# Part of a decoder block's input projection as a Strassen stage of its own, ahead of attention

## The chip, the cores and the metric

The kernel runs on one core of a Trainium2 chip. The metric is the time of one execution in microseconds on the device, as the median of several runs. The core has TensorE (PE: matmuls, with weight loads as PEld), VectorE (DVE), ScalarE (ACT), GpSimd (POOL) and queues that issue DMAs (SP's most of all). Each engine takes its instructions in the order in which they were put into its queue.

## The reference

One layer on 1024 tokens and 16 meta tokens of width 1024, in float32. Only the first part of it is changed, the mixer's input projection and what uses it:

```python
def hybrid_mixer(xn, w_in, conv_w_mix, w_proj_conv, w_proj_attn, b_gate, w_out):
    h = xn @ w_in                      # 1024 x 8192
    b_c, c_c, h_c, q, k, v, g_conv, g_attn = jnp.split(h, list(splits), axis=-1)
    y_conv = b_c * causal_dwconv(c_c * h_c, conv_w_mix)
    branch_conv = y_conv @ w_proj_conv
    o = stick_breaking_attention(q.reshape(hd), k.reshape(hd), v.reshape(hd))
    branch_attn = o.reshape(bsz, seq_len, D_ATTN) @ w_proj_attn
    gate_conv = jax.nn.sigmoid(g_conv + b_gate[0])
    gate_attn = jax.nn.sigmoid(g_attn + b_gate[1])
    merged = gate_conv * branch_conv + gate_attn * branch_attn
    return merged @ w_out
```

Attention has 16 heads of 64 and queries in blocks. For a query, the weight of an earlier key is the sigmoid of its score times the product of one minus sigmoid over all keys between them. Behind the mixer come a norm, a gated MLP (up and gate projections with 2816 channels each, a convolution over 3 tokens, a down projection), and a norm.

## The kernel before

Weights are laid out in blocks of 128 output channels; `w_in` has 64 such blocks: 8 each of b, c and h of the convolution, of q, k, v, and of two gates. Each fp32 value is split into a rounded part `hi` and a rest `lo` (`split`: ACT copies, DVE or POOL subtracts), and a product is three matmuls, hi x hi, hi x lo and lo x hi.

Start: nine `x_block` calls normalise 128 tokens each, transpose them on PE and split them into `xnT` (hi and lo, 8 channel blocks, 1040 tokens). Between them begin the first two blocks of the projection.

The class `Dense` works through a list of items, one item a block of weights. For each it loads `raw` (SP), makes `whi` (ACT) and `wlo` (POOL, four pieces), and goes in three chunks of some 342 tokens through 8 channel blocks, three matmuls each: 72 matmuls a block (lines 129 to 131). One step is three matmuls. A chunk's PSUM result goes to the item's `evac`. For q that is a copy on ACT and a cast and a subtraction on DVE for each of two heads (`qh`, `ql`), for k a copy and a subtraction (`kk`), for v a copy `vt`, later transposed to tokens (`vv`). Convolution items give `cc` and `yy`, gates `gt`; results that are used later are written to DRAM (`y_d`, `gc_d`, `ga_d`).

Attention runs over 8 pairs of heads, 2 heads, 3 groups `g` of three query blocks of 114. `stage1` makes scores `z` in PSUM (two buffers) for 114 queries and 128 to 1040 keys; ACT makes two sigmoids, `fl` and `be`; DVE scans `fl` along the keys (line 340); POOL multiplies it into `be` (line 346) and masks it (`affine_select`, line 348). `stage2` goes through the key blocks of a group: transposes of `be` on PE into `tp` (line 377, two buffers), ACT's copy `ah`, DVE's rest `al`, and two products `av` (lines 367, 368). A loop alternates the two stages by a table of costs, with `stage1` some 2500 units ahead, and spreads the projection's steps over them: `marks[p]` says how many items must be done when pair p is. Before, the list was v, q, k of pair 0, and then for each pair its three convolution items, one gate (four for the last) and v, q, k of the next pair. Five gates were left for after the loop.

The code is written in this order, but a scheduler moves instructions within each engine's queue at compile time; so what stands in a queue is shown below as it was compiled.

Then follow the products with `yT` and `oT` (the two branches), the output projection, the up and gate projections, and the down projection. The up and gate projections are already done in Strassen's scheme (in Winograd's form with 7 products), in pairs of weight blocks (lines 863 to 867), for tokens in even and odd columns.

Of the kernel before, what the change touches and what calls it, by code (L numbers as in the profile page):

```python
# [33 lines left out]
def block_kernel(ctx, tc, x, meta_tokens, g_pre_mix, w_in, channels, w_proj_conv,  # L34
# [32 lines left out]

    def rstd_of(small, ssq, n):
# [12 lines left out]
    class Dense:  # L81


        def __init__(self, pspool, items):
            self.ps = pspool
            self.items = items
            self.raw, self.hl = {}, {}
            self.i, self.gen, self.total, self.later = 0, None, 0, []

# [6 lines left out]

        def load(self, i):
            if i < len(self.items) and i not in self.raw and i not in self.hl:
# [5 lines left out]
        def prep(self, i):  # L104
            if i < len(self.items) and i not in self.hl:
# [35 lines left out]
        def step(self):  # L141
            while self.i < len(self.items):
# [17 lines left out]
    def col_block(w, c):  # L160
# [110 lines left out]

    def items_conv(cb):
        st = {}

        def evac_c(ci, a, n, ps):
            if ci == 0:
                st["c"] = work.tile([P, NT], F32, name="cc", tag="wk", bufs=4)
            nc.scalar.copy(st["c"][:, a - 12:a - 12 + n], ps)

        def evac_h(ci, a, n, ps):  # L280
            c = st["c"][:, a - 12:a - 12 + n]
            nc.vector.tensor_tensor(c, c, ps, op=ALU.mult)
            if ci == 2:
                st["y"] = work.tile([P, NT], F32, name="yy", tag="wk", bufs=4)
# [24 lines left out]
    gp = {"p": work, "n": 4}  # L309
# [91 lines left out]
    gate_items = [item_gate(1, ob) for ob in range(8)] + [item_gate(0, ob) for ob in range(8)]  # L401
    n_gate = [1, 1, 1, 1, 1, 1, 1, 4]
    items, marks = [], []
    items += [item_v(0), item_q(0), item_k(0)]
    gi = 0
    for p in range(NPAIR):
        items += items_conv(p)
        for _ in range(n_gate[p]):
            items.append(gate_items[gi])
            gi += 1  # L410
# [3 lines left out]
    items += gate_items[gi:]  # L414
    n_gates = len(items)
    dense = Dense(ps_mm, items)

    def start_items(x_block):
# [11 lines left out]
        chunk(0, 9)  # L430
        chunk(1, 9)
# [803 lines left out]
```

## Time and profile before

| | us |
|---|---|
| runs: median of 3 (lowest, highest) | 2024.38 (2021.74, 2027.97) |
| profiled execution, its own time | 2019.99 |
| its span in the profile | 2018.2 |
| PE busy in the span | 1968.4 |
| attention: first z to last av | 66.0 to 967 |

The profiled execution ran at a mean granted TensorE clock of 0.993. A row of groups shows line, engine, operation, out<-in, shape, count, then busy us and mean ns of one, then the engine's idle time before and what released it. A row of windows shows for each engine the busy us and, in brackets, the number of instructions. Rows of one tile give ns as least/median/greatest and the first and last start.

### The profile page before, as it was taken

How to read it: one execution, taken by the hardware profiler on the slowest of the kernel's cores; microseconds unless marked ns; L12 is line 12 of the kernel's file. 1: busy time of each engine (PE TensorE's matmuls, PEld its weight loads, DVE VectorE, ACT ScalarE, POOL GpSimd, SP SyncE). 2: the span in 40 equal slices, each digit the busy share in tenths (PEclk: the TensorE clock that was granted, in tenths of full speed). 3: DMA queues.
4: the chain of work that ended last, by engine and by line, in shares of the span. 5: the costliest groups of instructions: out<-in, count | busy, mean ns of one | idle time of the engine just before them, and what ended most of it. 6: DMA issues, size and time to landing. Idle time of an engine off the chain costs nothing.

```text
span 2018.2 us, 30990 instructions
## 1 busy us (share of the span) xinstructions
PE 1968.4 (98%) x12228; PEld 1857.0 (92%) x12228; DVE 1006.3 (50%) x1545; ACT 853.3 (42%) x1771; POOL 1022.7 (51%) x1062
## 2 busy tenths in 40 slices
PE   6999999999999999999999999979999999999997
PEld 6999999999999999999999999969988998888886
DVE  6445555555555555553341126874354445345546
ACT  5544555555454545555421123453443344321122
POOL 2643666565555646565223550345556565654353
PEclk9999999999999999999999999989999999999998
DMA  3111101111111111012664673303121212253223
GB/s 137 43 63 43 53 32 64 43 53 43 42 53 43 58 39 62 32 64 73 189 221 156 188 214 114 97 31 126 63 84 67 102 66 82 92 174 111 84 84 136
DMA packets 56174, 177.58 MB, mean 88 GB/s; under 512 B 12872, under 2 KB 12872, under 8 KB 56028
## 3 DMA queue, kind: packets, MB, share of 16 engines
q1 hardware_dynamic: 52704, 165.09, 24.5%
q10 hardware_dynamic: 3324, 10.50, 1.7%
q8 instruction: 96, 1.57, 0.3%
q14 instruction: 50, 0.41, 0.1%
HBM read 131.36 MB, written 44.21 MB: 87 GB/s over the span
## 4 chain that ended last, share of the span: by engine, by line
PE 87%; DVE 7%; ACT 2%; DMA 2%; POOL 1%; issue 1%; ACTq 0%; DVEq 0%; SPq 0%; POOLq 0%
PE mm L129 14%; PE mm L130 14%; PE mm L131 14%; PE st L863 7%; PE st L867 7%; PE st L865 7%; PE tp L377 3%; PE st L1157 3%; PE st L1155 3%; PE st L1156 3%; PE av L368 2%; PE av L367 2%; PE z L331 2%; PE z L330 2%; PE po L706 1%; PE po L708 1%
## 5 line engine op out<-in xcount | busy, mean ns | idle before, releaser
L129 PE MATMUL mm<-xnT,whi 128*128 128x342 f32 (+2 forms) x1536 | 505.5, 329 | 0.3 <-ACT xnT L65 0.2
L130 PE MATMUL mm<-xnT,whi 128*128 128x342 f32 (+2 forms) x1536 | 494.0, 322 | 0.5 <-DVE xnT L66 0.5
L131 PE MATMUL mm<-xnT,wlo 128*128 128x342 f32 (+2 forms) x1536 | 492.3, 320 | 0.0
L346 POOL TENSOR_TENSOR be<-be,fl 114x271 f32<-114x271 f32 (+14 forms) x288 | 206.0, 736 | 310.3 <-DVE fl L340 301.6
L113 POOL TENSOR_TENSOR wlo<-raw,whi 128x256 fp32r<-128x256 f32 x320 | 254.8, 828 | 208.2 <-ACT whi L110 207.3
L130 PEld LDWEIGHTS mm<-xnT,whi 128*128 128x128 f32 x1536 | 291.0, 189 | 2.1 <-DVE xnT L66 1.0
L129 PEld LDWEIGHTS mm<-xnT,whi 128*128 128x128 f32 x1536 | 290.2, 189 | 2.9 <-ACT xnT L65 0.8
L131 PEld LDWEIGHTS mm<-xnT,wlo 128*128 128x128 f32 x1536 | 290.0, 189 | 0.0
L340 DVE TENSOR_TENSOR_SCAN fl<-fl,upper 114x128 f32<-114x128 f32 (+2 forms) x144 | 214.4, 1490 | 112.2 <-ACT fl L332 64.0
L66 POOL TENSOR_TENSOR a_op<-raw,a_op 128x512 fp32r<-128x512 f32 (+1 forms) x136 | 193.7, 1437 | 87.9 <-ACT a_op L65 85.6
L66 DVE TENSOR_TENSOR al<-tp,ah 114x342 fp32r<-114x342 f32 (+3 forms) x288 | 128.3, 452 | 148.8 <-ACT ah L65 147.5
L65 ACT CAST ah<-tp 114x342 fp32r<-114x342 f32 (+3 forms) x288 | 113.0, 398 | 165.3 <-PE tp L377 157.0
L863 PE MATMUL st<-opT,a_op 128*128 128x258 f32 (+2 forms) x528 | 172.3, 326 | 3.2 <-ACT snap L878 1.8
L865 PE MATMUL st<-opT,a_op 128*128 128x258 f32 (+2 forms) x528 | 170.1, 322 | 2.6 <-DVE opT L66 1.7
L867 PE MATMUL st<-opT,a_op 128*128 128x258 f32 (+2 forms) x528 | 170.0, 322 | 0.0
L332 ACT ACTIVATE fl<-z 114x348 f32<-114x348 f32 (+10 forms) x240 | 111.4, 464 | 123.6 <-PE z L331 93.5
L65 ACT CAST a_op<-raw 128x512 fp32r<-128x512 f32 (+1 forms) x136 | 85.1, 634 | 156.0 <-DMA raw<-in_w_up_gate_dram 51.8
L1162 DVE TENSOR_TENSOR acc<-acc,st 128x512 f32<-128x512 f32 x144 | 98.5, 687 | 91.1 <-PE st L1157 91.1
L865 PE MATMUL st<-opB,a_op 128*128 128x512 f32 (+2 forms) x396 | 127.6, 322 | 0.0
L863 PE MATMUL st<-opB,a_op 128*128 128x512 f32 (+2 forms) x396 | 127.6, 322 | 0.0
L867 PE MATMUL st<-opB,a_op 128*128 128x512 f32 (+2 forms) x396 | 127.2, 321 | 0.0
L377 PE MATMUL tp<-ident,be 114*114 114x114 f32 (+1 forms) x720 | 118.5, 262 | 4.1 <-DVE al L66 3.4
(168 smaller groups left out, 4320.5 us busy)
## 6 DMA issues: line engine op xcount, KB each, us to landing
raw<-in_w_in_dram SPq DMA_DIRECT2D x64, 512.0 KB, 3.3
raw<-in_w_up_gate_dram SPq DMA_DIRECT2D x44, 512.0 KB, 3.3
act_d<-owork SPq DMA_DIRECT2D x22, 512.0 KB, 4.3
araw<-act_d SPq DMA_DIRECT2D x22, 512.0 KB
raw<-in_w_down_dram SPq DMA_DIRECT2D x22, 512.0 KB, 3.3
y_d<-yy SPq DMA_DIRECT2D x8, 513.0 KB
ga_d<-gt SPq DMA_DIRECT2D x8, 513.0 KB
o_d<-ot SPq DMA_DIRECT2D x8, 513.0 KB
```

Of the source, the lines that this page charges most:

```text
L65: nc.scalar.copy(hi, src)
L66: (lo_engine or nc.vector).tensor_tensor(lo, src, hi.bitcast(F32), op=ALU.subtract)
L113: nc.gpsimd.tensor_tensor(lo[:, c], raw[:, c], hi[:, c].bitcast(F32), op=ALU.subtract)
L129: nc.tensor.matmul(ps, wh, xh, start=(kb == 0), stop=False)
L130: nc.tensor.matmul(ps, wh, xl, start=False, stop=False)
L131: nc.tensor.matmul(ps, wl, xh, start=False, stop=(kb == KB - 1))
L340: nc.vector.tensor_tensor_scan(fl[:, :nk][:, ::-1], fl[:, :nk][:, ::-1], upper[:, NT - nk:][:, ::-1], 1.0, op0=ALU.mult, op1=ALU.max)
L346: nc.gpsimd.tensor_tensor(be[:, a:e], be[:, a:e], fl[:, a + 1:e + 1], op=ALU.mult)
L377: nc.tensor.transpose(tp[:n, QB * j:QB * (j + 1)], blocks[j][0][:, k0:k0 + n], ident[:QB, :QB])
L863: nc.tensor.matmul(ps, wt[:, 0, k], xh, start=start and kb == 0, stop=False, skip_group_check=True)
L865: nc.tensor.matmul(ps, wt[:, 0, k], xl, start=False, stop=False, skip_group_check=True)
L867: nc.tensor.matmul(ps, wt[:, 1, k], xh, start=False, stop=stop and kb == 3, skip_group_check=True)
```

## The change

30 of the 64 blocks leave the list: the convolution's blocks 1 to 7 (21), all 8 of the second gate and one of the first. They are computed in 15 pairs of blocks in the same scheme of 7 products, as a stage between the start and attention. The scheme halves channels (two halves of 512) and tokens (two halves of 520, `HT`): B11, B21, B22 are quarters of `xnT` itself, T1 to T4 are differences of quarters, made once by `token_ops`; A11, A12, A22 and S1 to S4 are made for each pair from two blocks of weights by `weight_ops`. `strassen` runs the 7 products for 260 tokens at a time, 12 matmuls each, with ACT copying three of the partial sums (`snap`) and DVE adding them. A pair is computed for all 1040 tokens. The convolution's first block (c, h, b) is done the old way at the start, in place of v, q, k of pair 0, which now follow the stage. Beside attention stand the other v, q, k and three gates; four gates are left for after the loop. Pools of SBUF and PSUM are opened and closed for the stage.

The diff, cut to its core:

```diff
+ps0 = ctx.enter_context(ExitStack())
+ps_mm0 = ps0.enter_context(pool("ps_mm0", 4, space=PSUM))
+ps_tp0 = ps0.enter_context(pool("ps_tp0", 4, space=PSUM))
...
-    n_gate = [1, 1, 1, 1, 1, 1, 1, 4]
-    items, marks = [], []
+    n_gate = [0] * 7 + [3]
+    std_gates = [item_gate(0, ob) for ob in range(1, 8)]
+    items, marks = items_conv(0), []
+    n_early = len(items)
     items += [item_v(0), item_q(0), item_k(0)]
     for p in range(NPAIR):
-        items += items_conv(p)
         for _ in range(n_gate[p]):
...
+    def token_ops():
+        for kb in range(4):
+            a, b = wk_tile("xa"), wk_tile("xb")
+            nc.vector.tensor_tensor(a, xnT[:, 0, kb].bitcast(F32), xnT[:, 1, kb].bitcast(F32), op=ALU.add)
+            nc.gpsimd.tensor_tensor(b, xnT[:, 0, kb + 4].bitcast(F32), xnT[:, 1, kb + 4].bitcast(F32),
+                                    op=ALU.add)
+            e1, o1, e2, o2 = a[:, :HT], a[:, HT:], b[:, :HT], b[:, HT:]
+            sub(nc.vector, o1, o1, e1)
+            split_top("T1", kb, o1)
+            sub(nc.vector, o1, o2, o1)
+            split_top("T2", kb, o1)
+            sub(nc.vector, e1, o1, e1)
+            split_top("T3", kb, e1)
+            sub(nc.vector, e2, e2, o1)
+            split_top("T4", kb, e2)
+            yield
...
+    for i in range(2):
+        next(tops_gen)
+        start_chunk(i, 9)
     dense.i, dense.total = 2, 48
-    dense.until(3)
...
+    load_early(0)
+    prep = prep_early(0)
+    for k in range(3):
+        dense.chunk()
+        next(tops_gen, None)
+        next(prep)
+    dense.until(n_early)
...
+    for i in range(len(early_pairs)):
+        prep = iter(()) if last else prep_early(i + 1)
+        tiles = [wk_tile("su") for _ in range(2)]
+        for si in range(2):
+            n = HT // 2
+            j0 = si * n
...
+            for k, _ in enumerate(strassen(early_ops[i], moving, n, bank_s, snaps_e,
+                                           early_evac(i, tiles, j0, n))):
+                if (7 * si + k) % 2:
+                    next(prep, None)
...
+    psS.close()
+    t_ctx.close()
+    early_ctx.close()
+    psA = ctx.enter_context(ExitStack())
...
+    dense.until(n_early + 3)
```

`weight_ops` and the order of the 7 products are those of the up projection (`prep_pair`, `products`); `early_evac` adds a result into one of two tiles `su` of 1040 tokens, and `done_c`, `done_h`, `done_b` and `done_gate` finish a block: c x h on POOL and the three convolution taps, the product with b on DVE, the sigmoid on ACT, and the DMA.

The queues at three places. First DVE just behind the last split of `xnT` at the start. Before:

```order
L230 CAST qh_348<-mm_468 64x342
L231 TENSOR_TENSOR ql_350<-mm_468,qh_348 64x342
L230 CAST qh_347<-mm_553 64x342
L231 TENSOR_TENSOR ql_349<-mm_553,qh_347 64x342
L66 TENSOR_TENSOR vv_552<-tp_598,vv_552 128x8x64
```

Now (xa and xb are the sums hi + lo of a slice of xnT, tT1 to tT4 the token operands):

```order
L433 TENSOR_TENSOR xa_502<-xnT_86 128x1040
L433 TENSOR_TENSOR xa_544<-xnT_86 128x1040
L69 TENSOR_TENSOR xa_502<-xa_502 128x520
L69 TENSOR_TENSOR xa_544<-xa_544 128x520
L66 TENSOR_TENSOR tT1_498<-xa_502,tT1_498 128x520
L69 TENSOR_TENSOR xa_502<-xb_503,xa_502 128x520
L69 TENSOR_TENSOR xa_502<-xa_502 128x520
L69 TENSOR_TENSOR xb_503<-xb_503,xa_502 128x520
L66 TENSOR_TENSOR tT2_499<-xa_502,tT2_499 128x520
L66 TENSOR_TENSOR tT3_500<-xa_502,tT3_500 128x520
L66 TENSOR_TENSOR tT4_501<-xb_503,tT4_501 128x520
L66 TENSOR_TENSOR tT1_498<-xa_544,tT1_498 128x520
```

The evacuations of q, and v's split, have given way to the token operands; 45 rows pass from the first of these to the last split of T4, with the convolution of block 0 and the first weight sums among them.

Second, DVE at the three longest scans of a head in the middle of attention. Before:

```order
L395 TENSOR_TENSOR ot_4879<-av_5438,ot_4879 64x342
L340 SCALAR_TENSOR_TENSOR fl_5502<-fl_5502,upper_93 114x812
L230 CAST qh_5460<-mm_5472 64x342
L231 TENSOR_TENSOR ql_5462<-mm_5472,qh_5460 64x342
L230 CAST qh_5461<-mm_5472 64x342
L231 TENSOR_TENSOR ql_5463<-mm_5472,qh_5461 64x342
L340 SCALAR_TENSOR_TENSOR fl_5540<-fl_5540,upper_93 114x926
L230 CAST qh_5460<-mm_5533 64x342
```

Now:

```order
L66 TENSOR_TENSOR vv_8321<-tp_8322,vv_8321 128x8x64
L399 TENSOR_TENSOR ot_8331<-av_8288,ot_8331 64x342
L66 TENSOR_TENSOR vv_8321<-tp_8347,vv_8321 128x8x64
L66 TENSOR_TENSOR vv_8321<-tp_8368,vv_8321 114x2x64
L344 SCALAR_TENSOR_TENSOR fl_8354<-fl_8354,upper_4080 114x812
L344 SCALAR_TENSOR_TENSOR fl_8380<-fl_8380,upper_4080 114x926
L231 CAST qh_8429<-mm_8343 64x342
L232 TENSOR_TENSOR ql_8431<-mm_8343,qh_8429 64x342
L344 SCALAR_TENSOR_TENSOR fl_8406<-fl_8406,upper_4080 114x1040
L231 CAST qh_8430<-mm_8343 64x342
L232 TENSOR_TENSOR ql_8432<-mm_8343,qh_8430 64x342
L66 TENSOR_TENSOR al_8456<-tp_8451,ah_8455 128x342
```

The work on DVE is the same, but the split `al` of the next group's first key block stands right behind it. PE has 28 projection matmuls between the last transpose before this piece and the transposes for that `al`.

Third, PE in the products of a group. Before:

```order
L377 MATMUL tp_5753<-ident_61,be_5411 114x114
L367 MATMUL av_5714<-ah_5730,vv_4081 128x342
L368 MATMUL av_5714<-al_5731,vv_4081 128x342
L129 MATMUL mm_5710<-xnT_92,whi_5581 128x344
L130 MATMUL mm_5710<-xnT_92,whi_5581 128x344
L131 MATMUL mm_5710<-xnT_92,wlo_5582 128x344
```

Now:

```order
L381 MATMUL tp_8483<-ident_61,be_8267 114x114
L371 MATMUL av_8450<-ah_8466,vv_7388 128x342
L372 MATMUL av_8450<-al_8467,vv_7388 128x342
L371 MATMUL av_8450<-ah_8477,vv_7388 128x342
L335 MATMUL z_8530<-kk_7858,ql_7499 114x128
L381 MATMUL tp_8496<-ident_61,be_8245 114x114
L381 MATMUL tp_8496<-ident_61,be_8267 114x114
L372 MATMUL av_8450<-al_8478,vv_7388 128x342
L371 MATMUL av_8450<-ah_8487,vv_7388 128x342
L381 MATMUL tp_8508<-ident_61,be_8267 114x114
L372 MATMUL av_8450<-al_8488,vv_7388 128x342
```

Before, three steps of the projection and two more groups of transposes stand between the transposes `tp_5753` and the product on their split; now `al_8488`, the split of `tp_8483`, is used after other products, one score matmul and three transposes, with no projection between.

More of the change, by code (lines that the diff above doesn't have):

```diff
@@ L95, in flush, with limit @@
                 self.later.pop(0)[1]()
+        @property
+        def limit(self):
+            return len(self.items) if self.stop is None else self.stop
         def load(self, i):
-            if i < len(self.items) and i not in self.raw and i not in self.hl:
+            if i < self.limit and i not in self.raw and i not in self.hl:
                 w = self.items[i][0]
@@ L104, in prep @@
         def prep(self, i):
-            if i < len(self.items) and i not in self.hl:
+            if i < self.limit and i not in self.hl:
                 self.load(i)
@@ L444, in x_load @@
             n = P if b < 8 else 16
-            xt = work.tile([P, NT], F32, name="xt", tag="be", bufs=6)[:, :D]
+            xt = small.tile([P, D], F32, name="xt", tag="xt", bufs=5)
             if b == 0:
@@ new lines, in block_kernel, with prep_early, early_evac, evac @@
+    tmp_e = sring.tile([P, 512], F32, name="tmp_e")
+    snap_t = sring.tile([P, 3, HT // 2], F32, name="snap_e")
+    snaps_e = [snap_t[:, k] for k in range(3)]
+    def prep_early(i):
+        got = early_ops[i] = {}
+        yield from weight_ops(*early_raw.pop(i), got, ring1_tile, tmp_e)
+        load_early(i + 1)
+    def early_evac(i, tiles, j0, n):
+        left = [2, 2]
+        def evac(o, par, ps, s):
+            dst = tiles[o][:, par * HT + j0:par * HT + j0 + n]
+            if s is None:
+                nc.scalar.copy(dst, ps)
+            else:
+                nc.vector.tensor_tensor(dst, ps, s, op=ALU.add)
+            left[o] -= 1
+            if j0 and not left[o]:
+                _, k, done = early_pairs[i][o]
+                done(k, tiles[o])
+        return evac
@@ L478, in block_kernel @@
+    nc.gpsimd.affine_select(out=upper[:, NT - QB:], in_=upper[:, NT - QB:], pattern=[[-1, QB]],
+                            compare_op=ALU.is_gt, fill=1.0, base=0, channel_multiplier=1)
+    at_ctx = ctx.enter_context(ExitStack())
+    heads = at_ctx.enter_context(pool("heads", 3, "right"))
+    work = at_ctx.enter_context(pool("work", 2, "right"))
+    gp["p"], gp["n"] = work, 4
+    dense.until(n_early + 3)
     LAG = 2500.0
```

202 lines of the change are left out of this document (172 added, 30 removed).

## The prediction

> **What bounds the kernel now.** I read the page first, then the stretches of the span, then spacings of matmuls, then waits and costs inside the attention stretch. From the page, the busy line and the chain that ended last:
>
> ```profile
> PE 1968.4 (98%) x12228; PEld 1857.0 (92%) x12228; DVE 1006.3 (50%) x1545; ACT 853.3 (42%) x1771; POOL 1022.7 (51%) x1062
> PE 87%; DVE 7%; ACT 2%; DMA 2%; POOL 1%; issue 1%; ACTq 0%; DVEq 0%; SPq 0%; POOLq 0%
> ```
>
> TensorE is the bound. The span cut at the first score product (66), the last attention product (967), the first matmul on yT, the first of w_out, and the first of the down-projection:
>
> ```profile
> core 0: us, PE busy (x) PEld busy (x) DVE busy (x) ACT busy (x) POOL busy (x), PEclk, DMA share, GB/s
> 0.00:66.00 66.00, 49.65 (x301) 46.85 (x302) 37.81 (x92) 32.67 (x68) 16.83 (x27) 1.00 0.34 121
> 66.00:967.00 901.00, 895.55 (x5929) 875.85 (x5928) 481.18 (x692) 467.66 (x1068) 516.37 (x673) 1.00 0.14 49
> 967.00:1014.00 47.00, 47.00 (x302) 47.00 (x301) 12.45 (x25) 19.95 (x41) 11.54 (x16) 1.00 0.72 220
> 1014.00:1196.00 182.00, 180.67 (x1154) 180.39 (x1153) 41.86 (x87) 38.32 (x67) 83.44 (x95) 1.00 0.64 194
> 1196.00:1763.00 567.00, 554.34 (x3495) 508.69 (x3494) 296.75 (x423) 241.22 (x447) 277.52 (x195) 0.98 0.26 86
> 1763.00:2018.00 255.00, 241.19 (x1058) 198.23 (x1056) 136.25 (x226) 53.50 (x81) 117.00 (x56) 0.98 0.35 120
> ```
>
> In the attention stretch (second row) DVE, ACT and POOL are busy for 53%, 52% and 57% of 901 us: slack that the change will spend. How many of its matmuls are input projection, and all that PE waited for there:
>
> ```profile
> 66.00:967.00 901.00, 761.70 (x4090) 657.25 (x4090) 0.00 (x0) 0.00 (x0) 1.00 0.14 49
> PE tp L377 <- DVE al L66: 3.4, 5, 2.1
> PE z L330 <- ACT be L333: 1.3, 1, 1.3
> ```
>
> So attention costs PE almost no waiting today, because 4090 projection matmuls fill every gap.
>
> A matmul's duration overlaps the next one's, so its price is the spacing of starts. The two ends of the yT/oT stretch (342 columns, six groups of 192), and one pair of up-projection blocks in two halves of 258 and 256 columns, which is the new stage's form:
>
> ```profile
> L129 PE MATMUL mm<-yT,whi x192: 315/318/327, 1014.2 to 1103.9; 128*128 128x342 f32 x192
> L131 PE MATMUL mm<-oT,wlo x192: 313/318/322, 1104.7 to 1196.1; 128*128 128x342 f32 x192
> 1364.40:1384.60 20.20, 20.20 (x169) 20.08 (x169) 5.74 (x11) 7.12 (x15) 10.94 (x9) 1.00 0.43 154
> ```
>
> 1152 matmuls in 181.9 us are 158 ns each at 342 columns; 168 in 20.2 us are 120 ns at 257. The difference is 0.44 ns a column, so 260 columns cost 121.6 ns.
>
> **Matmuls replaced: -35 us.** Removed: 30 blocks x 72 x 158 ns = 341 us. Added: 15 pairs x 2 halves x 7 products x 12 = 2520 x 121.6 ns = 306 us. The columns fall by a ninth, since the scheme's eighth is partly lost to the 12 or 14 leading tokens that these blocks did not compute before. The row of the up-projection pair already holds the stage's usual small waits, so I take the operand work of each later pair at nothing: DVE and ACT are busy there 5.7 and 7.1 of 20.2 us, POOL 10.9. Were that cover gone, a pair would be held by POOL, which has half of its time free; c and h pairs add two products of 1040 there, still inside.
> The Trainium skill ("TensorE: Matmul & The Clock Gate", Back-to-back issue gap) gives sustained spacings of about 81 ns at 128 columns and 131 at 512, which would leave a narrow matmul much less cheap; an estimate from that page is 98 ns at 260 and 109 at 342, so the new stage would cost 12 us more than the old blocks instead of 35 less. The two rows above contradict it.
>
> **Token operands at the start: +15 us.** They can begin when xnT is complete and need both halves of all tokens. Rows for that place, the last xnT split on DVE, SBUF-to-SBUF subtractions of 1032 and 512, ACT's copy of 512, and the first score product:
>
> ```profile
> L66 DVE TENSOR_TENSOR xnT<-tp,xnT x18: 203/682/693, 10.8 to 45.4; 128x512 fp32r<-128x512 f32 x16, 128x64 fp32r<-128x64 f32 x2
> 1308.32 1.22 DVE L775 TENSOR_TENSOR xr<-xr 128x1032 f32<-128x1032 f32 x1
> L775 DVE TENSOR_TENSOR raw<-raw x44: 682/694/1792, 1197.6 to 1740.3; 128x512 f32<-128x512 f32 x44
> L65 ACT CAST a_op<-raw 128x512 fp32r<-128x512 f32 x132 | 80.9, 621 | 149.1 <-DMA raw<-in_w_up_gate_dram 51.8 <-DVE raw L775 47.1 <-PE st L867 31.9
> L330 PE MATMUL z<-kk,qh x240: 220/323/418, 66.0 to 942.2; 128*114 128x348 f32 x24, 128*114 128x292 f32 x16, 128*114 128x406 f32 x16, 128*114 128x128 f32 x8
> ```
>
> The same 216 projection matmuls (c, h, b of block 0 in place of v, q, k of pair 0) take PE to about 66 us, one product without a token operand to 67.5. In DVE's new order the last slice of T1 has 36 instructions ahead of it from 45.6 us: 4 additions of 1040 x 1.22, 26 half-width ones x 0.70, 2 convolution taps x 1.34 and 4 small ones, together 28 us, so T1 is whole at 73.6, T2 3.5 us later. PE then stands 6 us before S1*T1 and 2 us before S2*T2: 8 us at least. POOL's four sums of 1040 and seven lo parts in the same 30 us stretch DVE's two-input operations (the 694 ns row reaches 1792). If every subtraction, ACT copy (0.62) and lo part ran one after another, 16 x 2.0 us + 4.9 us + 6 us of other work would end near 89 us and cost 21 us, with POOL's collisions up to 36. Nearest is the interleaved order, with some stretching: 15. Behind the waiting products stands the whole stage, so all of it counts. Closing and opening PSUM and SBUF pools twice: 2 us (bounds 0 and 4: at each of the two a last evacuation and a split, some 0.5 us each below, may stand open with their waits).
>
> **Attention beside less work: +42 us.** 2520 matmuls are gone from here or are no longer filler; by the new order 1785 projection matmuls stand between first score and last product instead of 4089. Attention's own PE time is 901 - 4090 x 0.158 = 255 us, so PE needs 255 + 282 = 537 us. What the other engines lose:
>
> ```profile
> L282 DVE TENSOR_TENSOR cc<-cc,mm 128x342 f32<-128x342 f32 (+1 forms) x24 | 12.3, 512 | 16.9 <-PE mm L131 16.8
> L289 DVE TENSOR_TENSOR yy<-yy,mm 128x342 f32<-128x342 f32 x24 | 12.0, 498 | 1.7 <-PE mm L131 1.7
> L204 DVE SCALAR_TENSOR_TENSOR yy<-cc,par,yy 128x1026 f32<-128x1026 f32 x8 | 11.1, 1385 | 0.0
> L203 DVE SCALAR_TENSOR_TENSOR yy<-cc,par,yy 128x1026 f32<-128x1026 f32 x8 | 10.7, 1339 | 11.8 <-ACT yy L202 11.8
> 66.00:967.00 901.00, 187.17 (x228) 1.00 0.14 49
> 66.00:967.00 901.00, 59.65 (x57) 1.00 0.14 49
> ```
>
> (The last two are POOL's wlo and ACT's whi; 1785/4090 of them stay.) DVE keeps 481 - 46 = 435 us, 81% of 537; ACT 468 - 34 = 434, 81%, the convolution's own copies still in it; POOL 516 - 105 = 411, 77%. All are in-order queues with two transpose buffers and two score buffers between them, and the load is not even. The costs of one burst:
>
> ```profile
> L340 DVE TENSOR_TENSOR_SCAN fl<-fl,upper 114x1040 f32<-114x1040 f32 x16 | 40.1, 2508 | 16.3 <-POOL be L346 9.7 <-ACT fl L332 6.5
> L340 DVE TENSOR_TENSOR_SCAN fl<-fl,upper 114x926 f32<-114x926 f32 x16 | 35.2, 2200 | 11.7 <-issue 9.0 <-ACT fl L332 2.4
> L340 DVE TENSOR_TENSOR_SCAN fl<-fl,upper 114x812 f32<-114x812 f32 x16 | 30.9, 1932 | 23.9 <-issue 14.4 <-ACT fl L332 9.6
> L340 DVE TENSOR_TENSOR_SCAN fl<-fl,upper 114x698 f32<-114x698 f32 x16 | 30.3, 1893 | 3.9 <-POOL be L346 2.1 <-ACT fl L332 1.7
> L340 DVE TENSOR_TENSOR_SCAN fl<-fl,upper 114x584 f32<-114x584 f32 x16 | 23.1, 1442 | 15.1 <-POOL be L346 9.7 <-ACT fl L332 2.8 <-POOL wlo L113 2.6
> L340 DVE TENSOR_TENSOR_SCAN fl<-fl,upper 114x470 f32<-114x470 f32 x16 | 18.5, 1157 | 10.4 <-ACT fl L332 10.4
> L230 DVE CAST qh<-mm 64x342 fp32r<-64x342 f32 x48 | 24.6, 512 | 21.6 <-ACT qh L229 20.9
> L231 DVE TENSOR_TENSOR ql<-mm,qh 64x342 fp32r<-64x342 f32 x48 | 24.6, 512 | 0.6
> L395 DVE TENSOR_TENSOR ot<-av,ot 64x342 f32<-64x342 f32 x48 | 24.3, 507 | 67.9 <-ACT ot L394 67.9
> L66 DVE TENSOR_TENSOR vv<-tp,vv 128x512 fp32r<-128x512 f32 x16 | 10.9, 681 | 17.6 <-ACT vv L65 17.5
> L66 DVE TENSOR_TENSOR al<-tp,ah 114x342 fp32r<-114x342 f32 x144 | 74.1, 514 | 89.3 <-ACT ah L65 88.4
> ```
>
> In the order piece with the three longest scans, DVE has, between two al, 2 vv x 0.68 + ot 0.51 + scans 1.93 + 2.20 + 2.51 + 4 evacuations of q x 0.51 = 10.6 us. PE has there 28 projection matmuls x 0.158 = 4.4, 14 score matmuls over 5556 columns at the same spacing 2.6, and about 1.2 of transposes and products: 8.2 us. PE is 2.4 us ahead and finds its transposes' buffers full. One unit later: 4 x 0.51 + 0.51 + scans 1.16 + 1.44 + 1.89 = 7.0 us against 21 x 0.158 + 1.6 + 0.6 = 5.5, so 1.5. That is 3.9 us a head pair, and 27 us for the seven pairs with a following q. Before, such a burst had over twice the projection work. A second term is the chain of one key block, which now stands bare. Its transposes and ACT's copy, where projections were scarce at the end:
>
> ```profile
> 951.68 0.46 PE L377 MATMUL tp<-ident,be 114*114 114x114 f32 x3
> 952.17 0.45 ACT L65 CAST ah<-tp 114x342 fp32r<-114x342 f32 x1 [0.80 <-PE tp L377]
> L348 POOL TENSOR_SCALAR_AFFINE_SELECT be<-be x144: 280/283/2386, 70.5 to 948.1; 114x114 f32<-114x114 f32 x144
> ```
>
> From the first transpose to the end of al: 0.49 + 0.45 + 0.51 = 1.45 us. In the new PE order the product on that al comes about 1.5 us of PE work later, in the tightest place, so any queueing on ACT or DVE (a pair of sigmoids, a scan) goes through to PE. For 288 key blocks I take 50 ns, 15 us. Bounds of the whole term: 0 if bursts are bridged by the buffers; at the top 90, if half of all bursts and a quarter us of each key block are lost.
>
> **Sum.** 2020.0 (the profiled execution; its span is 2018.2) - 35 + 15 + 2 + 42 = 2044. The profiled execution lies 4.4 us below the median of the runs shown, 2024.4, so a median of 2048. Work after the attention is the same; 228 projection matmuls remain behind it, not 300, and still cover the first yT loads.
>
> **Rivals.** (A) Attention keeps pace: the buffers bridge each burst and it loses 5 us, the start 10: 2020 - 35 + 10 + 2 + 5 = 2002, as a median 2006, faster. It decides below some 18 us of stalls in attention. For it: two short waits of PE in 901 us. Against: 81% of DVE in bursts that exceed PE's. (B) Scans and POOL exclude each other: the affine select's row, 283 ns median and 2386 at most, the length of a scan, shows POOL standing through one. The six long scan sizes are 178 us, with POOL's 411 they make a chain of 589, 52 above PE's 537; with the 27 of the bursts, 2020 - 35 + 15 + 2 + 79 = 2081, median 2085. Against: by the new order a block's transposes come some 13 us of PE work after its scores, so POOL may queue, and POOL's sum already holds part of its standing. The Trainium skill ("SBUF — State Buffer", Who interferes with whom) calls this an exclusive lock for the whole instruction; by that rule B's chain is the right one, and the trace agrees at this row. (C) The token chain is serial: +21 over the forecast, 2069. (D) Narrow matmuls do not get cheaper than 158 ns: 2520 x 0.158 = 398, +92, median 2140; the 20.2 us row excludes it, 1 in 100.
>
> **Chances.** Forecast 0.58, its own range 2030 to 2075; A 0.20; B 0.14; C 0.07; D 0.01. What can be told from no change is about 0.3%, 6 us. Faster by that: most of A, 0.17. Within: the rest of A and the forecast's low edge, 0.12. Slower: 0.71. The range 2008 to 2092 cuts off half of A and half of B's upper side.
>
> **What would show it.** In the changed profile: a new stage of 15 pairs at 20.4 us; PE idle 8 to 25 us before the first product on T1, released by DVE; an attention stretch of 560 to 600 us with PE waits on al, ah and z in tens of us, DVE near 76% busy. I am wrong if that stretch lies under 555 us, if a pair takes over 21 us, or if the first product on T1 starts before 70 us.

## The result, and the profile after

The changed kernel takes 2200.76 us (median of 4 runs, 2199.22 to 2206.11), the kernel before 2025.78 on the same chip: a ratio of 1.0871, with a 95% interval of 1.0845 to 1.0897. It is slower, as forecast, but by 175 us and not by 24, and outside the range. The profiled execution took 2201.01 us, with a span of 2199.3 and a mean granted clock of 0.963 (0.993 before). One of the ten executions of before_fl3 below took 3899 us, against 2019 to 2030 for the others, and is left out.

From the page after, the busy line and the chain that ended last. TensorE stands at 92% and not 98, and its share of the chain fell from 87% to 53; DVE, POOL and ACT came in:

```profile
PE 2012.9 (92%) x12588; PEld 1865.7 (85%) x12588; DVE 1113.1 (51%) x1696; ACT 917.5 (42%) x1943; POOL 1103.5 (50%) x1058
PE 53%; DVE 10%; POOL 9%; DMA 6%; ACT 6%; issue 3%; DVEq 0%; ACTq 0%; POOLq 0%; SPq 0%
```

The same span in windows (columns as before: the stretch, its length, busy us of PE, PEld, DVE, ACT, POOL, then clock). Rows: PE standing before the first Strassen product, the Strassen stage, v, q, k of pair 0, attention, the gates behind it, the rest:

```profile
68.00:89.80 21.80, 0.10 (x1) 0.00 (x0) 21.80 (x27) 7.31 (x13) 9.51 (x5) 0.60 0.00 0
89.80:421.40 331.60, 314.19 (x2522) 311.71 (x2523) 113.94 (x169) 118.67 (x236) 160.45 (x116) 0.96 0.25 74
421.40:457.00 35.60, 35.58 (x227) 35.25 (x227) 9.90 (x19) 10.87 (x22) 9.55 (x13) 1.00 0.28 75
457.00:1152.50 695.50, 599.80 (x3629) 549.42 (x3628) 431.39 (x628) 398.28 (x980) 414.86 (x545) 0.93 0.08 27
1152.50:1188.00 35.50, 35.50 (x228) 35.50 (x227) 10.81 (x23) 16.50 (x35) 8.48 (x12) 1.00 0.68 212
1188.00:2199.30 1011.30, 978.76 (x5702) 887.57 (x5700) 472.36 (x739) 333.64 (x598) 476.38 (x346) 0.99 0.36 115
```

Against the prediction's sum, whose span is 2042: attention 695.5 for 579, the stage 331.6 for 306.4, the first Strassen product at 89.8 for about 82, the work behind attention 1047 for 1040. Together that is 157 us, and 116 of them are attention. There PE was busy for 600 us and idle for 96, at a clock of 0.93. What was waited for in that stretch (engine, line, releaser: us in total, times, longest):

```profile
POOL be L350 <- DVE fl L344: 188.0, 45, 9.9
ACT ah L65 <- PE tp L381: 107.5, 147, 3.6
ACT fl L336 <- POOL be L350: 81.8, 32, 3.5
DVE fl L344 <- ACT fl L336: 79.2, 75, 4.1
DVE al L66 <- ACT ah L65: 58.7, 108, 2.0
PE z L334 <- ACT be L337: 43.4, 24, 2.9
PE av L371 <- ACT ah L65: 28.6, 22, 2.6
PE tp L381 <- DVE al L66: 22.7, 30, 1.2
```

The last three rows are PE's own waits, 94.7 of its 96 us. The third row is a wait for a buffer: ACT may not write `fl` because POOL still reads the `fl` of two blocks earlier, and `fl` has two buffers. All of ACT's other work stands behind it. Once, in the timeline (rows picked out of it; start, duration, instruction, in brackets the idle time before it and its releaser):

```profile
638.81 0.46 ACT L336 ACTIVATE fl<-z 114x350 f32<-114x350 f32 x1 [1.81 <-POOL be L350]
640.07 1.86 DVE L344 TENSOR_TENSOR_SCAN fl<-fl,upper 114x698 f32<-114x698 f32 x1 [1.68 <-ACT fl L336]
640.19 0.73 ACT L65 CAST ah<-tp 128x342 fp32r<-128x342 f32 x2
640.73 0.42 PE L371 MATMUL av<-ah,vv 128*128 128x342 f32 x1 [1.45 <-ACT ah L65]
641.96 0.82 DVE L66 TENSOR_TENSOR al<-tp,ah 128x342 fp32r<-128x342 f32 x2
642.62 0.41 PE L381 MATMUL tp<-ident,be 114*114 114x114 f32 x1 [1.16 <-DVE al L66]
```

ACT waits 1.81 us for POOL; the four sigmoids come first, then the late `ah`, for which PE has stood 1.45 us; meanwhile a scan has got in front of `al` on DVE, and PE stands another 1.16. Then the clock falls:

```profile
639.00:642.60 3.60, 1.01 (x5) 0.47 (x4) 2.50 (x3) 2.97 (x7) 3.45 (x5) 0.96 0.00 0
642.60:646.00 3.40, 3.38 (x16) 3.34 (x17) 0.89 (x3) 1.73 (x4) 3.12 (x6) 0.54 0.02 5
```

In the kernel before the same wait is there. It stood in its trace, and I had read only the waits of PE:

```profile
ACT fl L332 <- POOL be L346: 18.5, 19, 2.6
```

### The profile page after: what moved, and what is told of

It is laid out like the page before. It is cut to its first block, busy times and chain, and to the rows that moved or that the text cites. A ratio compares the mean times of both kernels' runs of the same rounds, so it can differ in the third digit from the quotient of the medians.

```text
span 2199.3 us, 32361 instructions
## 1 busy us (share of the span) xinstructions
PE 2012.9 (92%) x12588; PEld 1865.7 (85%) x12588; DVE 1113.1 (51%) x1696; ACT 917.5 (42%) x1943; POOL 1103.5 (50%) x1058
## 4 chain that ended last, share of the span: by engine, by line
PE 53%; DVE 10%; POOL 9%; DMA 6%; ACT 6%; issue 3%; DVEq 0%; ACTq 0%; POOLq 0%; SPq 0%
PE mm L139 5%; PE mm L137 5%; PE st L1110 5%; PE mm L138 5%; PE st L1114 4%; PE st L1112 4%; POOL be L350 4%; DVE fl L344 3%; PE st L1402 3%; PE st L1404 3%; PE st L1403 3%; PE tp L381 3%; POOL a_op L66 2%; PE av L372 2%; ACT fl L336 2%
## 5 line engine op out<-in xcount | busy, mean ns | idle before, releaser
L350 POOL TENSOR_TENSOR be<-be,fl 114x271 f32<-114x271 f32 (+14 forms) x288 | 244.7, 870 | 209.8 <-DVE fl L344 188.0
L137 PE MATMUL mm<-xnT,whi 128*128 128x342 f32 (+2 forms) x816 | 279.3, 343 | 2.1 <-ACT whi L118 2.0
L138 PE MATMUL mm<-xnT,whi 128*128 128x342 f32 (+2 forms) x816 | 272.2, 334 | 1.0 <-DVE xnT L66 1.0
L139 PE MATMUL mm<-xnT,wlo 128*128 128x342 f32 (+2 forms) x816 | 271.7, 333 | 0.6 <-POOL wlo L121 0.6
L344 DVE TENSOR_TENSOR_SCAN fl<-fl,upper 114x128 f32<-114x128 f32 (+2 forms) x144 | 208.1, 1455 | 80.8 <-ACT fl L336 79.2
L121 POOL TENSOR_TENSOR wlo<-raw,whi 128x256 fp32r<-128x256 f32 x200 | 146.0, 761 | 204.5 <-ACT whi L118 189.6
L69 DVE TENSOR_TENSOR raw<-raw 128x512 f32<-128x512 f32 x74 | 72.4, 978 | 213.7 <-POOL a_op L66 106.3
L137 PEld LDWEIGHTS mm<-xnT,whi 128*128 128x128 f32 x816 | 161.6, 198 | 5.1 <-ACT whi L118 2.3
L138 PEld LDWEIGHTS mm<-xnT,whi 128*128 128x128 f32 x816 | 162.4, 199 | 2.7 <-DVE xnT L66 1.5
L139 PEld LDWEIGHTS mm<-xnT,wlo 128*128 128x128 f32 x816 | 162.6, 199 | 0.9 <-POOL wlo L121 0.9
L66 POOL TENSOR_TENSOR s_op<-raw,s_op 128x512 fp32r<-128x512 f32 x90 | 128.3, 1437 | 58.3 <-ACT s_op L65 49.5
L336 ACT ACTIVATE fl<-z 114x348 f32<-114x348 f32 (+10 forms) x240 | 112.1, 467 | 107.7 <-POOL be L350 81.8
L563 PE MATMUL st<-tT,s_op 128*128 128x260 f32 x480 | 138.8, 289 | 17.4 <-ACT snap_e L573 15.2
```

The source lines that it names most:

```text
L66: (lo_engine or nc.vector).tensor_tensor(lo, src, hi.bitcast(F32), op=ALU.subtract)
L137: nc.tensor.matmul(ps, wh, xh, start=(kb == 0), stop=False)
L138: nc.tensor.matmul(ps, wh, xl, start=False, stop=False)
L139: nc.tensor.matmul(ps, wl, xh, start=False, stop=(kb == KB - 1))
L336: nc.scalar.activation(fl[:, c0:c0 + n], z, AF.Sigmoid, scale=-0.125)
L344: nc.vector.tensor_tensor_scan(fl[:, :nk][:, ::-1], fl[:, :nk][:, ::-1], upper[:, NT - nk:][:, ::-1], 1.0, op0=ALU.mult, op1=ALU.max)
```

## The experiments

My theory was the ring (R): two buffers of `fl` tie ACT to POOL. Rivals: too little filler (F), whatever the buffers; the clock (C), a price of its own for pauses; POOL and DVE shutting each other out (P), rival B of the prediction; and something in the new program's pools (N). An attention stretch is taken from first score product to last attention product, in the one profiled execution of each run. The executions of one run differ by up to 13 us, so 10 us of difference in a stretch show little by themselves.

| run | median us | ratio to before, 95% | attention, us | its PE busy |
|---|---|---|---|---|
| after | 2200.8 | 1.0871, 1.0845 to 1.0897 | 695.5 | 599.8 |
| plain | 2183.2 | 1.0797, 1.0771 to 1.0823 | 700.2 | 606.9 |
| fl3 | 2106.1 | 1.0421, 1.0399 to 1.0442 | 606.1 | 560.6 |
| nopool | 2090.2 | 1.0333, 1.0309 to 1.0356 | 585.9 | 554.2 |
| junk | 2247.2 | 1.1117, 1.1086 to 1.1148 | 738.5 | 668.5 |
| dose6 | 2082.8 | 1.0285, 1.0260 to 1.0310 | 652.0 | 619.7 |
| dose6_fl2 | 2145.5 | 1.0604, 1.0582 to 1.0626 | 712.0 | 634.6 |
| fl3_tp3 | 2105.5 | 1.0416, 1.0397 to 1.0436 | 595.7 | 549.9 |
| fl3_deep | 2102.5 | 1.0388, 1.0368 to 1.0408 | 597.0 | 551.5 |
| fl3_qact | 2110.5 | 1.0428, 1.0410 to 1.0446 | 605.5 | 559.4 |
| fl3_noscan | 2071.0 | 1.0231, 1.0214 to 1.0247 | 568.0 | 553.2 |
| before_fl3 | 2022.1 | 0.9999, 0.9986 to 1.0013 | 903.6 | 897.4 |

**plain: the same blocks ahead of attention, without Strassen's scheme.**

```diff
 # the kernel before
+    items, marks = [item_v(0), item_q(0), item_k(0)], []
+    for p in range(NPAIR):
+        items += items_conv(p)
+    items += gate_items[:9]
...
-    dense.until(3)
+    dense.until(n_early)
```

> The kernel before, with the same 30 blocks done ahead of attention as plain items (72 matmuls a block) and not in Strassen's scheme; attention then has the same 1785 projection matmuls beside it as the changed kernel. Theory F (too little filler): attention takes about 695 us as in the changed kernel, and the whole is 66 + 341 (2160 matmuls at 158 ns) + 36 for v, q, k less what the start already has, + 695 + 36 + 1005: 2160 to 2190. Rival N (something of the new program, its pools or banks, spoils attention): attention 540 to 600 us, the whole 2020 to 2075.

2183, and attention takes 700 us with the same 81.8 us of ACT's wait:

```profile
ACT fl L332 <- POOL be L346: 81.8, 33, 3.5
PE z L330 <- ACT be L333: 42.0, 23, 2.9
```

So the loss needs neither Strassen's scheme nor its pools: N falls. The new stage itself, with its start, is no better than the same blocks done plainly: attention begins at 457 us with it and at 438.8 here, and the whole is 17.6 us apart (15 by the ratios).

**fl3: three buffers of fl.**

```diff
-            fl = work.tile([P, NT], F32, name="fl", tag="fl")[:QB]
+            fl = work.tile([P, NT], F32, name="fl", tag="fl", bufs=3)[:QB]
...
-    gp["p"], gp["n"] = work, 4
+    gp["p"], gp["n"] = work, 3
```

(`vt` and `ot`, which share the tag `wk`, also go to three.)

> The changed kernel with three buffers of fl instead of two (and three of wk). Theory R (the ring: ACT's first sigmoid of a block waits for POOL's multiply two blocks back, 81.8 us in the changed kernel's trace, and the copies ah queue behind it): that wait falls under 30 us, attention from 695 to 580 to 640, the whole 2090 to 2145. Theories C (the clock that falls after PE's pauses) and F (too little filler) alone: within 15 us of 2200, the wait moves to another place.

2106: one more buffer gives back 95 us (91 by the ratios, since the two runs had different chips), 89 of them in attention. Of the 89, 50 are idle time of PE (96 to 46) and 39 are faster matmuls (599.8 to 560.6 busy). ACT's wait is all but gone, PE's on scores is 7.3 us in place of 43.4, and the clock is back at 0.99:

```profile
457.50:1063.60 606.10, 560.59 (x3627) 514.63 (x3626) 445.27 (x628) 397.40 (x979) 443.37 (x545) 0.99 0.09 31
```

The two largest waits of that kind left in it:

```profile
ACT fl L336 <- POOL be L350: 4.4, 5, 1.6
PE tp L381 <- DVE al L66: 33.9, 37, 1.7
```

R is right.

**nopool: without POOL's multiply and mask of be.**

```diff
-                w = -(-(nk - 1) // (-(-nk // 384)))
-                for a in range(0, nk - 1, w):
...
-                nc.gpsimd.affine_select(out=be[:, nk - QB:nk], in_=be[:, nk - QB:nk],
```

> The changed kernel without POOL's multiply and mask of be (the weights are the bare sigmoids). It bounds what POOL can cost by standing late in the chain or by standing through scans. Theory P (POOL is the late link, by the ring or by exclusion with scans): attention 540 to 600 us, the whole 2045 to 2105. If ACT, DVE and the transposes' chain are slow by themselves (F): attention above 650, the whole above 2155.

2090, with two buffers. All that POOL's late link can cost is 110 us of attention, and one buffer took back 89 of them. So at most 20 are left for P's exclusion beyond the ring. How much of the 89 is there only because the collisions make POOL hold `fl` longer (see the last section) no run separates: fl3 keeps the collisions, and this run drops them together with the ring's last link.

**junk: one more matmul in each projection step.**

```diff
+                    for _ in range(self.extra):
+                        nc.tensor.matmul(ps[:32], zt[0], xh, start=False, stop=False)
                     nc.tensor.matmul(ps, wl, xh, start=False, stop=(kb == KB - 1))
```

> The changed kernel with one more matmul in each step of the projection beside attention (zero weights, so it adds nothing): 595 more of 342 columns, 94 us of PE time at 158 ns. Of attention's 695 us, 537 are PE's need at full clock, 96 idle, 62 slower clock. Theory C (the clock's fall is a price of its own): the work fills pauses, the clock stays up, attention 635 to 670, the whole 2140 to 2175. Theories R and P (other engines set the pace): attention stays at 690 to 700 and the whole at 2195 to 2205. If PE's stalls do not absorb it: +94, 2295.

Neither: 2247. Attention grew by 43 us for 94 us of matmuls. Its window, and ACT's wait in it:

```profile
463.50:1202.00 738.50, 668.51 (x4222) 600.67 (x4221) 433.32 (x628) 398.36 (x979) 413.72 (x545) 0.96 0.08 26
```

```profile
ACT fl L341 <- POOL be L355: 75.4, 32, 3.5
```

The clock rose from 0.93 to 0.96 and idle time fell from 96 to 70 us, but the ring's wait stayed. Filler that is spread evenly paid for half of itself, 51 of 94 us: 26 in less idle time, the other 25 in faster matmuls. So the lower clock is a price that adds to the stalls (about 47 us of the changed kernel's attention), but not one large enough to pay for filler: C as the main cause falls.

**dose6 and dose6_fl2: six gates back beside attention, with three and with two buffers.** Both also have two gates at the start and the late ACT work of the runs below; 11 pairs are left.

```diff
-    n_gate = [0] * 7 + [3]
+    n_gate = [1] * 6 + [0, 3]
```

> Three buffers of fl, both mends of the stage (gates at the start, the deferred ACT work), and six more gate blocks taken out of the stage (11 pairs are left) and done one beside each of the first six head pairs of attention: PE's need there goes from 537 to 605 us. Theory F (too little filler): 606 us of attention had 69 of stalls with three buffers, which the 68 us of filler mostly fill: attention 618 to 640, the whole 2106 - 21 - 20 - 61 + 12 to 34: 2016 to 2038. Rival (stalls are bursts that more filler does not fill): attention 665 to 680, the whole 2063 to 2080.

> The same as the run before, with two buffers of fl. Theory R (the ring holds ACT whatever stands beside it, as the extra matmuls showed, which cost half of their time): attention 695 + 34, about 730, the whole 2110 to 2140. Rival (the filler hides the ring as the kernel before suggests): within 15 us of the run with three buffers.

652 us and 712 us of attention. With three buffers the 68 us of filler cost 46, which lies between F (618 to 640 us of attention) and its rival (665 to 680): F explains a part. The whole, 2082.8, is above both ranges, which also counted on the late ACT work; that brought nothing (fl3_defer below). With two buffers the ring still costs 60 us: attention is below the 730 that R gave, the whole, 2145.5, a little above its range.

ACT's wait in dose6_fl2:

```profile
ACT fl L336 <- POOL be L350: 69.7, 39, 4.1
```

**before_fl3: the kernel before, with three buffers of fl** (and three of `wk`).

> The kernel before with three buffers of fl (and three of wk, for space). Its trace had ACT waiting for POOL's multiply for 18.5 us, hidden behind projection work: PE was busy for 895.5 of attention's 901 us. Theory H (the ring cost nothing there): 2017 to 2030, the same as before. Rival (the ring cost something already, or the one buffer of wk less costs): outside of it, by more than 6 us.

0.9999. ACT's wait goes from 18.5 to 5.4 us and nothing follows:

```profile
ACT fl L332 <- POOL be L346: 5.4, 7, 0.8
```

So the ring's price goes from nothing beside 4089 projection matmuls to 60 us beside 2217 and 89 beside 1785.

**What remains with three buffers: fl3_tp3, fl3_qact, fl3_noscan, fl3_deep.** All are on top of fl3; deep includes tp3:

```diff
 # tp3
-    ps_mm = psA.enter_context(pool("ps_mm", 3, space=PSUM))
+    ps_mm = psA.enter_context(pool("ps_mm", 2, space=PSUM))
-    ps_tp = psA.enter_context(pool("ps_tp", 2, space=PSUM))
+    ps_tp = psA.enter_context(pool("ps_tp", 3, space=PSUM))
 # qact
-                nc.vector.tensor_copy(hi[other, c], ps[own])
+                nc.scalar.copy(hi[other, c], ps[own])
 # noscan
-                nc.vector.tensor_tensor_scan(fl[:, :nk][:, ::-1], fl[:, :nk][:, ::-1],
...
 # deep
-            if len(pend) > 2:
+            if len(pend) > 3:
```

> Three buffers of fl, and in PSUM three transpose buffers and two projection buffers instead of two and three. With three buffers of fl alone attention took 606 us against PE's need of 537, and PE's largest wait was tp on al, 33.9 us in 37 waits. Theory K (the chain of a key block, transposes, ah, al, with two buffers carries the rest, as the prediction's 42 us had it): that wait falls under 15 us, attention 560 to 590, the whole 2060 to 2090. Rival (bursts of DVE and ACT longer than a buffer bridges, or the projection's own evacuations, which have one buffer less): within 10 us of 2106 or above it.

The total stayed, as the rival had it, and the wait moved from tp to av, so a chain's latency was only carried on:

```profile
PE av L372 <- DVE al L66: 32.4, 38, 1.7
```

> Three buffers of fl, and the second copy of q (48 of 512 ns on DVE, 24.6 us, of which seven eighths lie in attention) on ACT. Theory D (DVE's bursts at the three longest scans, the prediction's 27 us): attention 580 to 595, the whole 2080 to 2095. Rival (ACT is as near to its limit in the burst, since ah and the sigmoids queue there): within 6 us of 2106, or slower.

No gain. PE's wait on `al` falls from 33.9 to 27.3 us, so q's copies do stand in front of it, but its wait on ACT's `ah` rises from 3.6 to 9.0 and that on scores from 7.3 to 8.7. The sum stays at 45 us: ACT had no room either, as the rival had it. The first two in this run:

```profile
PE tp L381 <- DVE al L66: 27.3, 29, 1.2
PE av L371 <- ACT ah L65: 9.0, 10, 1.3
```

> Three buffers of fl, and DVE's scans left out (POOL multiplies by the bare sigmoids): 222 us of DVE's work go. It bounds what the scans cost by standing in DVE's queue ahead of al and of POOL's multiply. Theory L (the scans are what remains of attention's loss with three buffers, 606 us against a need of 537): attention 540 to 565, the whole 2040 to 2066. Rival (the chain of scores, sigmoids, transposes and copies loses it without them): above 585, the whole above 2085.

568 us, just above what L expected (565): 38 of the 606 go with the scans, and PE's wait on `al` goes too. The 38 hold all that a scan does: its place in DVE's queue, POOL's wait for it, and its collisions with POOL. The window, and the wait:

```profile
457.10:1025.10 568.00, 553.23 (x3627) 511.96 (x3626) 226.09 (x484) 393.90 (x980) 318.17 (x545) 1.00 0.10 33
```

```profile
PE av L369 <- DVE al L66: 0.9, 5, 0.2
```

The window says more. At a clock of 1.00 PE is busy for 553 us (550 in fl3_tp3), so some 550 and not 537 is its need here: the prediction's 255 + 282 was 13 to 16 too low. Below I take 553.

> Three transpose buffers (two for the projection), and the products of a key block issued three blocks behind its transposes instead of two. A third transpose buffer alone moved PE's wait from tp on al (33.9 us) to av on al (32.4 us) and left the time. Theory L (al comes late by the length of a scan, which one more key block in flight bridges): the wait on al falls under 15 us, attention 570 to 592, the whole 2070 to 2093. Rival (PE's pace is set by DVE's sum over a burst, not by the latency of one scan): within 10 us of 2105.

2102.5. The waits on `al` sum to 35 us over tp and av as before. The intervals of fl3, fl3_tp3 and fl3_deep overlap, so one more block in flight is worth at most a few us. That the scans cost 38 us is shown; by which way (the queue on DVE, the sum of a burst, POOL's wait and the collisions) is open.

**The start: fl3_start.**

```diff
+    items += [item_gate(1, 7), item_gate(0, 0)]
     n_early = len(items)
```

> Three buffers of fl, and two gate blocks taken out of the stage (14 pairs are left) and done the old way at the start, behind the convolution's first block and ahead of the stage: 144 matmuls at 158 ns, 22.8 us, while DVE makes the token operands. Theory S (PE stood for the token operands and the PSUM bank behind them, 68 to 89.8 us): the first Strassen product again at 89 to 93 us, one pair less, the whole 2080 to 2092. Rival (the token operands come later by as much, since evacuations and weight splits of the two blocks share ACT, DVE and POOL): first product past 100 us, the whole 2098 to 2110.

2093.7, ratio 1.0351 (1.0328 to 1.0374): 12 us less and not 21. The first product moved to 97 us, so the gates' 22.8 us cover about 15. Both numbers lie between S and its rival, nearer to S.

**The stage: fl3_defer, fl3_tap, fl3_quart, fl3_dveprod.** ACT at the end of an h pair in the changed kernel; PE stands at that place for 4.1 us:

```profile
133.48 0.38 ACT L660 COPY su<-st 128x260 f32<-128x260 f32 x1 [0.75 <-PE st L567]
135.34 1.15 ACT L203 ACTIVATE su<-su,par 128x1026 f32<-128x1026 f32 x1 [1.48 <-POOL su L608]
138.92 1.15 ACT L203 ACTIVATE su<-su,par 128x1026 f32<-128x1026 f32 x1 [2.42 <-POOL su L608]
139.98 0.36 ACT L573 COPY snap_e<-st 128x260 f32<-128x260 f32 x1
```

The edits, each on top of fl3 (defer: `taps` is called in the next pair; tap: `on_pool` puts it on POOL; quart: the product is called per quarter of h):

```diff
 # defer
-            conv3(y[:, :NQ], c[:, T0 - 2:], NQ, lambda k: w_mix(k, cb))
+            behind.append(taps)
 # tap, in conv3
+            nc.gpsimd.tensor_scalar(dst, src[:, 2:2 + n], wt(2), None, op0=ALU.mult)
 # quart, in early_evac
+                nc.gpsimd.tensor_tensor(c, c, dst, op=ALU.mult)
 # dveprod
-            nc.gpsimd.tensor_tensor(c, c, y, op=ALU.mult)
+            nc.vector.tensor_tensor(c, c, y, op=ALU.mult)
```

> Three buffers of fl, and in the Strassen stage the convolution's first tap (ACT) and the gate's sigmoid (ACT) are issued in the middle of the next pair's first half instead of at once. In the changed kernel's trace ACT waits there for POOL's product of 1040 (14.5 us in 7 waits), the copies snap queue behind it, and the first half of such a pair takes 13 to 17 us and not 10. Theory Q (that queue on ACT lengthens the stage): the halves come to 10 to 11 us, the stage from 332 to 308 to 318, the whole 2082 to 2094. Rival (the loads of weights, the weight operands on POOL or the clock by itself): the stage stays above 325, the whole 2099 to 2110.

2108.7, nothing: in the compiled program ACT's queue there has the same order, so the scheduler undid the edit, and Q was not tested by it.

> Three buffers of fl, and in the Strassen stage the convolution's first tap on POOL behind its own product, no longer on ACT. Putting the tap later in the program had moved nothing: ACT's queue had the same order, and ACT waited there for POOL's product as before (14.5 us in 7 waits). Theory Q (ACT's wait for POOL's product holds the copies snap, and PE behind them): the first halves of 13 to 17 us come to 10 to 11.5, the stage from 332 to 308 to 318, the whole 2082 to 2094. Rival (POOL, which also makes the lo parts of the next weights, now holds the products by as much): the stage above 325, the whole 2099 to 2112.

2121.1, worse by 15. POOL's tap takes 2.9 us in the median, DVE waits 30 us for it, and PE for DVE:

```profile
PE st L566 <- DVE su L665: 32.3, 9, 9.1
DVE su L207 <- POOL su L204: 30.0, 7, 7.0
```

> Three buffers of fl, and POOL's product of c and h made in quarters of 260 columns as the quarters of h arrive, instead of whole tiles of 1040 at the pair's end. Theory Q (ACT waits with its first tap for POOL's two products, 14.5 us, with the copies snap behind): what is left at the end of a pair is one short product, the first halves of 16 to 17 us come to 11 to 13, the stage from 332 to 312 to 322, the whole 2085 to 2096. Rival (POOL and DVE slow each other, or the clock): the stage above 327, the whole above 2100.

2104.6; the stage takes 329 us, and ACT still waits 12.1 us for the quarters, which stand behind lo parts on POOL.

> Three buffers of fl, and the product of c and h on DVE instead of POOL, in whole tiles. With quarters on POOL the first halves after an h pair still took 15 to 16 us, since POOL's quarters stood behind the lo parts of the next weights and ACT's tap waited for the last of them. Now ACT's tap waits for DVE alone, and in ACT's queue the first copy snap stands ahead of the second tap. Theory Q (ACT's queue holds the copies): those halves come to 10.5 to 13 us, the stage from 332 to 311 to 321, the whole 2086 to 2097. Rival (DVE, with the product, both taps and the additions of the results, now holds them): the stage above 327, the whole above 2100.

2095.5, ratio 1.0365 (1.0349 to 1.0380), the stage 319.5 us. ACT's queue at the same place:

```profile
134.19 1.16 ACT L203 ACTIVATE su<-su,par 128x1026 f32<-128x1026 f32 x1 [0.20 <-DVE su L608]
135.25 0.35 ACT L573 COPY snap_e<-st 128x260 f32<-128x260 f32 x1
136.45 1.16 ACT L203 ACTIVATE su<-su,par 128x1026 f32<-128x1026 f32 x1 [0.84 <-DVE su L608]
```

The copy starts 4.7 us earlier, and the halves after an h pair take 11 to 13 us. PE's wait on the copies in the stage, in fl3 and here:

```profile
PE st L563 <- ACT snap_e L573: 15.2, 5, 4.1
PE st L563 <- ACT snap_e L573: 1.5, 1, 1.5
```

Q is right: 12 of the stage's 25 us were ACT waiting for POOL ahead of its copies. Some of what was won comes back as a wait on DVE's additions (2.2 us in the changed kernel, 8.6 here).

**Together: best14, best11.** The first has fl3, deep, quart and the gates at the start; the second fl3, deep, dveprod, the gates at the start and dose6's 11 pairs.

> Together: three buffers of fl, three transpose buffers and products three blocks behind, the product in quarters, and two gates done at the start (14 pairs). If each is worth what its own theory says: 2106 - 12 - 14 - 22, 2050 to 2070. If the products three blocks behind and the quarters are worth nothing: 2085 to 2098.

> Together: three buffers of fl, products three key blocks behind, two gates at the start, six gates beside attention (11 pairs are left), the product of c and h on DVE. The run with 11 pairs took 2083; by theory Q 12 to 18 less, by deeper products 0 to 4 less: 2060 to 2072. If neither is worth anything here: 2078 to 2086.

2092.1 and 2076.0 (ratio 1.0262, 1.0237 to 1.0286). Both miss their first sum, and 2092.1 lies in the second range of best14, 2076.0 just under that of best11: the parts do not add up. A pair still takes 22 us in both (307.7 us for 14, 242.1 for 11). No version that I ran beats the kernel before.

## Why the prediction was wrong

**The step that failed: "Attention beside less work: +42 us".** It measured 158, beyond its upper bound of 90. By the rows above: 16 are PE's need, 553 for 537; about 47 are slower matmuls, 599.8 busy for 553 at a clock of 0.93; 96 are idle. By cause, in the order in which I removed them: the ring 89 (fl3), the scans 38 (fl3_noscan), and 31 that PE's need (16) and the last 15 us of idle make up. Of the two terms that I had put there, DVE's bursts at the long scans (27) are of the right kind and too small, since 38 go with the scans. The chain of a key block (15) is not borne out: one more transpose buffer and one more block in flight left the time. Whether the last 15 us of idle are it is open. What I had left out was the largest, and it could be read: a wait of 18.5 us on ACT for a buffer, while PE waited for nothing. I listed what PE waits for, and what each engine is busy for, but not what the other engines wait for among themselves. A block came every 901 / 144 = 6.3 us and would have come every 537 / 144 = 3.7, so with two buffers one `fl` may be held for 12.5 us before and for 7.5 after. Its sigmoids, scan and multiplies alone hold it for (111.4 + 214.4 + 206.0) / 144 = 3.7 us in the mean in the trace of before, the longest scan for 2.5 us, and ACT's other sigmoids, `al` on DVE and `wlo` on POOL stand between. By the waits of the two traces 12.5 us were nearly always enough for all of that (18.5 us of waiting), and 7.5 were not (81.8).

**Rival B** named POOL and the scans, and gave 2085 by adding up busy times. It named the right engines, and not the buffer that ties them: nopool leaves at most 20 us beyond the ring, and what the collisions add to the ring itself is open.

**Matmuls replaced, -35.** The spacing was right: undisturbed halves take 10.02 to 10.07 us, two 20.1. The stage took 331.6, 22.1 us a pair, where over 21 was the prediction's own sign of being wrong. The first halves after an h pair took 13.6 to 17 us: "I take the operand work of each later pair at nothing" failed at the seven convolution products, where POOL had room by its sum but ACT's queue had none. Of the 25 us, 17 are idle time of PE (331.6 - 314.2), the rest mostly lower clock (0.96).

**Token operands, +15.** PE stood for 21.7 us and the first product came at 89.8 for 82. The size was near by luck, the wait was another: not T1, but the product that needs no token operand, which wanted a PSUM bank that DVE had not emptied. DVE was busy for all of that stretch with 27 instructions, most of them for the token operands, and its last split of one ended at 91.0:

```profile
89.81 0.58 PE L563 MATMUL st<-xnT,s_op 128*128 128x260 f32 x1 [21.71 <-DVE yy L293]
```

**Work after attention** was 7 us longer than forecast. The stretch from yT on is 1004 us before, 1005 to 1011 in before_fl3, fl3, plain and after; the cause is open.

## What to carry to other kernels

Before you take filler away from beside a pipeline, list the waits of the engines that are not the bound: a wait for a buffer that costs nothing now is the first thing to reach the path. Multiply the time between two blocks that you expect after the change, not that of today, by the number of a ring's buffers, and compare it with the time that one buffer is held. An engine with half of its time free can still be the wrong place, if what stands behind it in another engine's queue is what PE waits for.

## What the runs showed of the hardware

Two pauses of PE, 1.45 and 1.16 us, with 1.01 us of work in the 3.6 us around them, were followed by 3.4 us at a granted clock of 0.54. The Trainium skill ("TensorE: Matmul & The Clock Gate", What's actually happening) has half rate follow an idle window of about 3.4 us; here the engine was not idle for the whole of it. In the changed kernel's attention the clock fell to half 22 times, for 96 us in all. In the 3.41 us before each fall PE was busy for 0.97 to 1.56 us, and its longest pause there was 0.98 to 2.45 us. The falls lie a whole number of 3.41 us apart, and in the 153 other such stretches at full clock PE was busy for at least 1.93 us. So pauses of a microsecond are enough, where they leave PE busy for less than half of such a stretch. In fl3 and junk the two kinds overlap, between 1.67 and 2.34 us, so no sharp limit is shown. Attention's mean clock was 0.93 with 96 us of idle time, 0.96 with 70 (junk), and 0.99 with 46 (fl3).

POOL's operations stretch over DVE's scans and the scans over POOL's. With three buffers of `fl` the multiply takes 1015 ns in the mean, and a scan 1562:

```profile
L350 POOL TENSOR_TENSOR be<-be,fl 114x271 f32<-114x271 f32 (+14 forms) x288 | 286.3, 1015 | 97.3 <-DVE fl L344 85.4 <-ACT be L337 8.2 <-PE z L335 3.0
L344 DVE TENSOR_TENSOR_SCAN fl<-fl,upper 114x128 f32<-114x128 f32 (+2 forms) x144 | 222.4, 1562 | 32.9 <-ACT fl L336 19.2 <-POOL be L352 8.8 <-POOL be L350 2.7
```

In the changed kernel, with two buffers, the multiply takes 870:

```profile
L350 POOL TENSOR_TENSOR be<-be,fl 114x271 f32<-114x271 f32 (+14 forms) x288 | 244.7, 870 | 209.8 <-DVE fl L344 188.0 <-PE tp L381 10.0 <-ACT be L337 8.2
```

Without scans (fl3_noscan) it takes 703:

```profile
L347 POOL TENSOR_TENSOR be<-be,fl 114x271 f32<-114x271 f32 (+14 forms) x288 | 197.9, 703 | 166.8 <-ACT be L337 159.3 <-PE z L335 4.6
```

And without POOL's work (nopool) a scan takes 1384:

```profile
L344 DVE TENSOR_TENSOR_SCAN fl<-fl,upper 114x128 f32<-114x128 f32 (+2 forms) x144 | 197.4, 1384 | 32.6 <-ACT fl L336 30.7
```

The Trainium skill ("SBUF — State Buffer", Who interferes with whom) calls it an exclusive lock; the trace agrees that they collide. Once the ring had a third buffer, the price in time was at most 20 us (nopool); what it adds to the ring with two buffers is not shown.
